# Eight conv tiles as block-product pairs in the early stage, and low parts of the scan's weights by accumulating DMA

## The chip, the cores and the metric

The kernel runs on one core of a Trainium2 chip. Its engines are TensorE (PE in the profile, with its weight loads as PEld), VectorE (DVE), ScalarE (ACT), GpSimd (POOL) and SyncE (SP); SP, ACT and POOL also issue DMAs, each from a queue of its own. Each engine works through its instructions in order. The metric is the device time of one execution in microseconds. A measurement of this kernel can tell a difference of about 0.3% from none.

## The reference

One layer of a hybrid encoder on 1024 tokens of 1024 channels. Cut to what matters here:

```
u     = rms_norm(x) * (1 + scale1) + shift1
gl, cb, cc, cx, z, xbc, dt = split(u @ w_in)
y_conv = cb * causal_conv3(cc * cx)                  # 8 tiles of 128 channels
xbc   = silu(causal_conv4(xbc) + b)                  # 32 tiles: xs, bs, cs
y     = ssd_scan(xs * dt, dt * a, bs, cs) + d_skip * xs   # 8 groups of 4 heads
y     = group_rms(y * silu(z)) * w
merged = sigmoid(gl0) * (y_conv @ w_conv_out) + sigmoid(gl1) * (y @ w_ssm_out)
x     = x + gate1 * (merged @ w_o)
x     = x + gate2 * (relu(u2 @ w_up)^2 @ w_down);  out = rms_norm(x)
```

`y_conv` needs three projections for each of its eight 128-channel tiles: `cc`, `cx` and `cb`. The scan needs four `xbc` tiles for each of its eight groups.

## The kernel before

All matrix work is done in float32 split into a high and a low part, each in the fast float32 format: a product is three matmuls (high x high, high x low, low x high). Weights come in tiles of 128 partitions x 1024 from HBM. `load_w` (L91 to L98) loads one into `wraw` (three buffers, queue of SP), casts it on ScalarE to the high part `whi`, and subtracts on VectorE for the low part `wlo` (four buffers each).

There are two ways to do a projection. `proj` (L119) takes one weight tile and all 1024 tokens: 8 row blocks x 2 halves of 512 tokens x 3 products (`mm3`, L111), which is 48 matmuls of 512 columns. `strassen_pair` (L136) takes two weight tiles and makes 2 x 2 blocks of them and of `u`; seven block products of 12 matmuls each (`prod`, L141) give the two output tiles, 84 matmuls instead of 96. It needs sums and differences of the blocks of `u`, `T1` to `T4`, made once before the early stage and held in SBUF (pools `tk0` to `tk3`); the sums of weight blocks are made on VectorE for each pair (`s12`, `s34`).

The stages, in order:

- Start: `u` from `x` and the conditioning, and the first gate tiles.
- Early stage: pairs by `strassen_pair`. Gate tiles `gl`, then the 16 `z` tiles, then conv tiles 0 to 3 (L483 to L508): for two conv tiles, one pair each gives `cx` and `cc`, whose product `v` goes through the three taps (`taps`, L477), and a third pair gives the two `cb` tiles. Results go to DRAM, the conv tiles to `yc_d`. Then the `T` blocks are released.
- Scan stage: `proj_group(g)` (L561) makes the four `xbc` tiles of a group with `xbc_tile` (L547): `proj` of one weight tile, copy to `raw` behind three zero columns that POOL sets each time, four taps, silu. `ssd_group(g)` (L573) goes through 8 chunks of 128 tokens: matmuls A (L580 to L583), B (L603, L608) and C (L625), small steps on VectorE and ScalarE between them, and a state passed from chunk to chunk. At the end of a group `zs` is multiplied by the result and POOL stores it to `y_d` (L645). `finish` sums squares.
- The loop over groups (L692 on) issues `ssd_group(g)`, then `proj_group(g + 1)`, and for g = 1 to 4 `conv_tile` (L671): conv tiles 4 to 7, each by three `proj`, with its own `ccs` and `vv` from pool `pcf` (two buffers).
- After the scan: all eight conv tiles are read back from `yc_d` through `ccs` (L710), split, and projected by `w_conv_out` beside the last scan group; then the output projections, the merge, `w_o`, and the two parts of the MLP. The down projection makes some low parts another way (L961, L962): ScalarE writes -1 times the raw tile, rounded to the fast format, which is minus the high part, and POOL issues a DMA that adds the raw weights from HBM to it; what is left is the low part.

What is issued when on each engine is fixed at build time: a planner takes the instructions in the order of the program as priorities, with its own estimate of their durations, and lays each engine's order down. Work that comes later in the program fills the gaps of work that comes earlier. Buffers are handed on with waits (`reuse_waits`).

Of the kernel before, what the change touches and what calls it, by code (L numbers as in the profile page):

```python
# [8 lines left out]
F32 = mybir.dt.float32  # L9
F32R = mybir.dt.float32r  # L10
I32 = mybir.dt.int32
AF = mybir.ActivationFunctionType
ALU = mybir.AluOpType
# [3 lines left out]
P = 128  # L17
T = 1024
H = 512
# [3 lines left out]
NC_ = 8  # L23
EPS = 1e-6
RSQRT_SEED = 0x5F3759DF
NYE = 4
PARTS = ((0, 512, (1, 4, 6)), (512, 256, (1, 3, 4, 6)), (768, 256, (2, 5)))

LN1, LN2, FNORM = 0, 8, 16
# [9 lines left out]
def hybrid_trunk(tc, xT, par, hrows, crow, wada1, wada2, win, wdt, wco, wso, wo, wup, wdt_, wdn, out):  # L39
    nc = tc.nc  # L40
    pe, act, dve, pool, sp = nc.tensor, nc.scalar, nc.vector, nc.gpsimd, nc.sync

    def tt(o, a, b, op, eng=dve):
        return eng.tensor_tensor(out=o, in0=a, in1=b, op=op)  # L44

    def stt(o, a, s, b, op0, op1):
        return dve.scalar_tensor_tensor(out=o, in0=a, scalar=s, in1=b, op0=op0, op1=op1)  # L47
# [4 lines left out]
    hs = [slice(0, H), slice(H, T)]  # L52

    cp = tc.alloc_tile_pool(name="const", bufs=1)
    wp = tc.alloc_tile_pool(name="weights", bufs=4)
# [29 lines left out]
    yc_d = dp.tile([8, P, T], F32, name="yc_d")  # L85

    def load_raw(src):
        raw = wp.tile([P, T], F32, name="wraw", bufs=3)
        sp.dma_start(raw, src)
        return raw  # L90

    def load_w(src, raw=None, eng=dve):
        if raw is None:
            raw = load_raw(src)
        hi = wp.tile([P, T], F32R, name="whi")
        act.copy(hi, raw)  # L96
        lo = wp.tile([P, T], F32R, name="wlo")
        tt(lo, raw, hi.bitcast(F32), ALU.subtract, eng=eng)  # L98
        return hi, lo

    def split(hi, lo, src):
        act.copy(hi, src)
        tt(lo, src, hi.bitcast(F32), ALU.subtract)
# [7 lines left out]
    def mm3(outs, wh, wl, xh, xl, start, stop):  # L111
        for o, h_, l_ in zip(outs, xh, xl):
            pe.matmul(o, lhsT=wh, rhs=h_, start=start, stop=False)  # L113
            pe.matmul(o, lhsT=wh, rhs=l_, start=False, stop=False)  # L114
        for o, h_ in zip(outs, xh):
            last_mm[0] = pe.matmul(o, lhsT=wl, rhs=h_, start=False, stop=stop)  # L116

    def proj(w, xh, xl, nk=KT, base=0, halves=(0, 1), width=H):
        wh, wl = w  # L119
        ps = [mm.tile([P, H], F32, name="mm")[:, :width] for _ in halves]  # L120
        for k in range(nk):
            c0 = base + k * P
            mm3(ps, wh[:, c0:c0 + P], wl[:, c0:c0 + P], [xh[k][h] for h in halves], [xl[k][h] for h in halves],
                k == 0, k == nk - 1)
        return ps
# [122 lines left out]
    uh = [[up.tile([P, H], F32R, name=f"uh{k}{h}") for h in (0, 1)] for k in range(KT)]  # L248
    ul = [[up.tile([P, H], F32R, name=f"ul{k}{h}") for h in (0, 1)] for k in range(KT)]
# [16 lines left out]
    for h in (0, 1):  # L266
        ps = mm.tile([P, H], F32, name="mm")
# [50 lines left out]
    for h in (0, 1):  # L318
# [3 lines left out]
        ps = ps0.tile([P, H], F32, name="st")  # L322
# [43 lines left out]
    p0.release()  # L366
    p0x.release()
    ws = [load_w(win[f]) for f in (4, 5)]
    tks, X = [], {n: [] for n in ("11", "21", "22", "T1", "T2", "T3", "T4")}
    dc1 = dcs[:, 8:12]  # L370
# [23 lines left out]
    for h in (0, 1):  # L394
        ps = ps0.tile([P, H], F32, name="st")
# [6 lines left out]
    ps = ps0.tile([P, H], F32, name="st")  # L402
# [74 lines left out]
    def taps(o, v, f):  # L477
        w0 = CONVW + 3 * f
        act.mul(o, v[:, 2:2 + T], prm[:, w0 + 2:w0 + 3])
        for j in (1, 0):  # L480
            stt(o, v[:, j:j + T], prm[:, w0 + j:w0 + j + 1], o, ALU.mult, ALU.add)

    for f0 in range(0, NYE, 2):  # L483
        ys_ = []
        for f in (f0, f0 + 1):
            y = glp.tile([P, T], F32, name="glt")
            v = pe1.tile([P, T + 32], F32, name="wv", bufs=1)
            pool.memset(v[:, 0:2], 0.0)
            keep = {}

            def v_ev(i, h, src):
                if (i, h) == (1, 1):
                    keep[0] = src
                elif (i, h) == (0, 0):
                    act.copy(y[:, hs[0]], src)
                else:
                    tt(v[:, 2 + H * h:2 + H * h + H], src, keep[0] if h else y[:, hs[0]], ALU.mult)

            strassen_pair(pe1, win[17 + 3 * f], win[16 + 3 * f], X, v_ev)
            taps(y, v, f)  # L500
            ys_.append(y)

        def y_ev(i, h, src):
            tt(ys_[i][:, hs[h]], src, ys_[i][:, hs[h]], ALU.mult)

        strassen_pair(pe1, win[18 + 3 * f0], win[21 + 3 * f0], X, y_ev)
        for i in (0, 1):
            act.dma_start(yc_d[f0 + i], ys_[i])  # L508
# [5 lines left out]
    with tc.issue_after(last_mm[0].ins):  # L514
        strict = p0e.tile([P, P], F32, name="strict")
        tsc(strict, tri, -1.0, 1.0, ALU.mult, ALU.add)
        ps = ps1.tile([P, H], F32, name="st")
        pe.matmul(ps[:, :C2], lhsT=tri, rhs=z2, start=True, stop=True)
        act.copy(acum.rearrange("p c h -> p (c h)"), ps[:, :C2])
        ps = ps1.tile([P, H], F32, name="st")  # L520
        pe.matmul(ps[:, :C2], lhsT=strict, rhs=z2, start=True, stop=True)
        pe.matmul(ps[:, C2:2 * C2], lhsT=ones, rhs=z2, start=True, stop=True)
        v = p0e.tile([P, C2], F32, name="v")
# [4 lines left out]
        for h in (0, 1):  # L528
            ps = ps1.tile([P, H], F32, name="st")
# [11 lines left out]
    p2t = tc.alloc_tile_pool(name="p2t", bufs=2, reuse_waits="tile")  # L541
    pcf = tc.alloc_tile_pool(name="pcf", bufs=2, reuse_waits="tile")
    psA = tc.alloc_tile_pool(name="psA", bufs=2, space=PSUM)
    psB = tc.alloc_tile_pool(name="psB", bufs=1, space=PSUM)
    psC = tc.alloc_tile_pool(name="psC", bufs=1, space=PSUM)

    def xbc_tile(win_i, ci, dst):  # L547
        ps = proj(load_w(win[win_i]), uh, ul)
        raw = p2t.tile([P, T + 3], F32, name="raw")
        pool.memset(raw[:, 0:3], 0.0)  # L550
        for h in (0, 1):
            act.copy(raw[:, 3 + H * h:3 + H * h + H], ps[h])
        a = p2t.tile([P, T], F32, name="cacc")
        for h in (0, 1):
            act.activation(a[:, hs[h]], ps[h], AF.Identity, bias=hb[:, ci:ci + 1], scale=hw[:, 4 * ci + 3:4 * ci + 4])  # L555
        for j in (2, 1, 0):
            stt(a, raw[:, j:j + T], hw[:, 4 * ci + j:4 * ci + j + 1], a, ALU.mult, ALU.add)
        act.activation(dst, a, AF.Tanh)
        stt(dst, dst, 1.0, a, ALU.add, ALU.mult)

    def proj_group(g):  # L561
        pg = p2g[g % 2]
        xs = pg.tile([P, 2, T], F32, name="xs")
        bf = pg.tile([P, T], F32, name="bf")
        cf = pg.tile([P, T], F32, name="cf")
        b = gtile(g)
        xbc_tile(b + 0, 2 * g, xs[:, 0, :])
        xbc_tile(b + 1, 2 * g + 1, xs[:, 1, :])
        xbc_tile(b + 2, 16 + g, bf)
        xbc_tile(b + 3, 24 + g, cf)  # L570
        return xs, bf, cf
# [96 lines left out]
        tsc(r, r, 0.5, None, ALU.mult, ALU.bypass)  # L668
        act.dma_start(rst_d[4 * i:4 * i + 4].rearrange("g (c t) -> (g c) t", t=P), r)

    def conv_tile(f):  # L671
        ccs = pcf.tile([P, T], F32, name="ccs")
        v = pcf.tile([P, T + 2], F32, name="vv")
        pool.memset(v[:, 0:2], 0.0)
        cps = proj(load_w(win[16 + 3 * f]), uh, ul)
        for h in (0, 1):
            act.copy(ccs[:, hs[h]], cps[h])
        xps = proj(load_w(win[17 + 3 * f]), uh, ul)
        for h in (0, 1):
            tt(v[:, 2 + H * h:2 + H * h + H], xps[h], ccs[:, hs[h]], ALU.mult)  # L680
        taps(ccs, v, f)
        bps = proj(load_w(win[18 + 3 * f]), uh, ul)
        for h in (0, 1):
            tt(ccs[:, hs[h]], bps[h], ccs[:, hs[h]], ALU.mult)
        act.dma_start(yc_d[f], ccs)

    def drive(gen):
        try:
            next(gen)
            return None  # L690
        except StopIteration as e:
            return e.value  # L692
# [3 lines left out]
    for g in range(NG - 1):  # L696
        gen = ssd_group(g, *cur, prev)
        prev = None
        while prev is None:
            prev = drive(gen)  # L700
        cur = proj_group(g + 1)
        if g in (1, 2, 3, 4):
            conv_tile(NYE + g - 1)
    up.release()

    yy = tc.alloc_tile_pool(name="yy", bufs=8, side="right", reuse_waits="tile")
    yc = []
    for f in range(8):
        ccs = pcf.tile([P, T], F32, name="ccs")
        sp.dma_start(ccs, yc_d[f])  # L710
        y = yy.tile([P, 2, T], F32R, name="ys")
        split(y[:, 0, :], y[:, 1, :], ccs)
        yc.append(y)
# [6 lines left out]
    for f in range(8):  # L720
# [3 lines left out]
        ps = proj(load_w(wco[f]), ych, ycl)  # L724
# [9 lines left out]
    for b in range(4):  # L734
# [18 lines left out]
        for f in range(8):  # L753
            if f % 2 == 0:
                w = load_w(wso[b, f // 2])
            if b == 0:
# [5 lines left out]
                ps = proj(w, yh, yl, nk=4, base=(f % 2) * 512)  # L762
# [10 lines left out]
            ps = proj(w, yh, yl, nk=4, base=(f % 2) * 512)  # L773
# [30 lines left out]
    for h in (0, 1):  # L804
        st = Stats(p6, pst, pool, 7)
        for f in range(8):
            x_ = xp.tile([P, H], F32, name=f"x{f}{h}")
            sp.dma_start(x_, xT[f, :, hs[h]])
            ps, = proj(load_w(wo[f]), mh, ml, halves=(h,))
# [12 lines left out]
    for h in (0, 1):  # L822
        for i in range(4):
            ps, = proj(ws[i], u2h, u2l, halves=(h,))
# [82 lines left out]
    for f in range(8):  # L907
# [4 lines left out]
        ps = proj(w, hh, hl, nk=4, base=(f % 2) * 512)  # L912
# [9 lines left out]
    for s in range(3):  # L922
# [26 lines left out]
        for n, blk in enumerate((0, 2, 5, 4, 3, 1, 6)):  # L949
            t = operand([lambda q=q: stage(op_d[s, 2 * q:2 * q + 2, :, blk, :].rearrange("k p t -> p k t")) for q in (0, 1)])  # L950
            first = n in (0, 2, 3, 5)
            for q in (0, 1):
                wh = wp.tile([P, T], F32R, name="whi")
                wl = wp.tile([P, T], F32R, name="wlo")
                for i in (0, 1):
                    val, src = piece(n, 2 * q + i)
# [29 lines left out]
    for t0, tw, onpool in PARTS:  # L986
        h, o = t0 // H, t0 % H
# [3 lines left out]
        for f in range(8):  # L991
            ps, = proj(ws[f // 2], [[v[h][:, win_]] for v in hh], [[v[h][:, win_]] for v in hl],
                       nk=4, base=(f % 2) * 512, halves=(0,), width=tw)
# [83 lines left out]
```

## Time and profile before

| what | value |
|---|---|
| median of 3 runs | 2125.92 us (2124.54 to 2130.34) |
| the profiled execution | 2126.34 us |
| its span, first to last instruction | 2124.3 us |
| mean granted TensorE clock | 0.989 |
| last block products of the early stage | 482.75 us |
| first scan matmul (A of group 0) | 543.06 us |
| end of the store of group 6's `zs`, issue | 1119.02 us |

A row of a group reads: line, engine, operation, output <- inputs, shape, count | busy time, mean ns of one | idle time of its engine before it and what ended it. Line 44, 47 and 50 are helpers (`tt`, `stt`, `tsc`), so groups are told apart by the names of their tiles. In the timeline a row is start, duration, engine, line and operation, with the idle time before it in brackets. A PE row's duration is longer than the interval to the next, since matmuls are pipelined.

### The profile page before, as it was taken

Reading aid. Unit: us, or ns where it says so; the run is one execution under the profiler, and the core shown is the slowest. Engines: PE = TensorE matmul, PEld = TensorE weight load, DVE = VectorE, ACT = ScalarE, POOL = GpSimd, SP = SyncE. Lnnn points to the kernel's source line nnn. Section 1 sums busy time; section 2 is a strip of 40 time slices with the busy share of each in tenths; the row PEclk is TensorE's granted clock in tenths of the full one; section 3 lists DMA queues with packets and bytes.
Section 4 is the critical chain, followed back from the end, with each engine's and each line's share of the span. In section 5 each row is a group of like instructions: output and inputs, shape, how many; then the busy total and the mean of one; then the engine's idle time right before and its main releaser. Section 6 shows DMA issues by size and latency. Waiting matters only on the chain.

```text
span 2124.3 us, 26250 instructions
## 1 busy us (share of the span) xinstructions
PE 2089.6 (98%) x9776; PEld 1705.5 (80%) x9776; DVE 1474.3 (69%) x2278; ACT 927.4 (44%) x1554; POOL 152.3 (7%) x242
## 2 busy tenths in 40 slices
PE   7999999999999999999999999999999999999998
PEld 4778888888888887888877888888888888888887
DVE  7866888665786757576786558845866665668674
ACT  4433333224565636364664231233544454544432
POOL 0000000000000000000000000011000001232213
PEclk8999999999999999999999999999999999999998
DMA  8226554223133223232337586453144347988932
GB/s 302 80 100 200 189 189 165 71 80 122 60 100 110 85 90 85 95 115 80 104 121 262 189 299 201 159 203 124 65 164 159 145 162 261 304 241 254 275 77 80
DMA packets 133617, 327.32 MB, mean 154 GB/s; under 512 B 12481, under 2 KB 47681, under 8 KB 131954
## 3 DMA queue, kind: packets, MB, share of 16 engines
q1 hardware_dynamic: 98978, 202.76, 29.4%
q0 software_dynamic: 22240, 87.04, 12.9%
q10 hardware_dynamic: 12272, 35.85, 4.3%
q8 instruction: 77, 1.26, 0.2%
q14 instruction: 50, 0.41, 0.1%
HBM read 253.05 MB, written 72.55 MB: 153 GB/s over the span
## 4 chain that ended last, share of the span: by engine, by line
PE 82%; issue 10%; DVE 4%; DMA 2%; POOL 1%; ACT 1%; SPq 0%; DVEq 0%; POOLq 0%; ACTq 0%
PE mm L147 21%; PE mm L116 15%; PE mm L113 15%; PE mm L114 15%; PE mm L971 9%; PE B L603 2%; PE B L608 1%; PE C L625 1%; DMA wv<-in_wada 1%; DVE wada L294 1%; PE A L580 1%; DMA x<-in_xT 1%; POOL wv L418 1%; DVE ul L47 1%; DVE x L47 0%
## 5 line engine op out<-in xcount | busy, mean ns | idle before, releaser
L113 PE MATMUL mm<-uh,whi 128*128 128x512 f32 x768 | 303.0, 398 | 3.7 <-ACT uh L106 3.2
L114 PE MATMUL mm<-ul,whi 128*128 128x512 f32 x768 | 304.8, 397 | 0.0
L147 PE MATMUL mm<-t,whi 128*128 128x512 f32 x944 | 290.5, 390 | 0.9 <-DVE cq L44 0.9
L116 PE MATMUL mm<-uh,wlo 128*128 128x512 f32 x768 | 246.4, 396 | 1.9 <-DVE wlo L44 1.9
L96 ACT CAST whi<-wraw 128x1024 fp32r<-128x1024 f32 x101 | 106.1, 1050 | 261.9 <-PE mm L114 219.9
L44 DVE TENSOR_TENSOR wlo<-wraw,whi 128x1024 fp32r<-128x1024 f32 (+1 forms) x167 | 186.6, 1118 | 37.4 <-ACT whi L96 31.3
L147 PEld LDWEIGHTS mm<-t,whi 128*128 128x128 f32 x944 | 176.9, 188 | 39.1 <-DVE cq L44 2.4
L971 PE MATMUL mm<-op,whi 128*128 128x512 f32 x672 | 207.2, 389 | 1.0 <-DVE y L47 0.9
L147 PE MATMUL mm<-t,wlo 128*128 128x512 f32 x472 | 183.0, 389 | 0.0
L113 PEld LDWEIGHTS mm<-uh,whi 128*128 128x128 f32 x768 | 144.5, 189 | 35.6 <-ACT uh L106 4.9
L116 PEld LDWEIGHTS mm<-uh,wlo 128*128 128x128 f32 x768 | 144.9, 189 | 32.2 <-DVE wlo L44 2.3
L114 PEld LDWEIGHTS mm<-ul,whi 128*128 128x128 f32 x768 | 145.0, 189 | 29.4 <-issue 0.9
L113 PE MATMUL mm<-ys,whi 128*128 128x512 f32 x384 | 148.9, 397 | 2.3 <-DVE gt L47 1.8
L44 DVE TENSOR_TENSOR wlo<-s,whi 128x1024 fp32r<-128x1024 f32 (+1 forms) x114 | 112.0, 995 | 54.4 <-ACT whi L152 53.6
L114 PE MATMUL mm<-ys,whi 128*128 128x512 f32 x384 | 149.1, 396 | 0.0
L971 PEld LDWEIGHTS mm<-op,whi 128*128 128x128 f32 x672 | 126.0, 188 | 28.1 <-ACT whi L957 1.3
L47 DVE SCALAR_TENSOR_TENSOR cacc<-raw,hw,cacc 128x1024 f32<-128x1024 f32 x96 | 122.9, 1280 | 27.6 <-ACT cacc L555 27.2
L147 PE MATMUL mm<-s,whi 128*128 128x512 f32 x448 | 138.3, 389 | 0.7 <-ACT cu L170 0.7
L971 PE MATMUL mm<-op,wlo 128*128 128x512 f32 x336 | 130.7, 389 | 0.0
L597 ACT ACTIVATE seg<-acb,acum 128x128 f32<-128x128 f32 x256 | 81.9, 392 | 98.7 <-PE B L603 88.6
L47 DVE SCALAR_TENSOR_TENSOR y<-mm,mcol,y 128x512 f32<-128x512 f32 (+1 forms) x100 | 69.4, 706 | 77.6 <-PE mm L971 39.4
L116 PE MATMUL mm<-ys,wlo 128*128 128x512 f32 x384 | 122.5, 394 | 0.0
(280 smaller groups left out, 4080.9 us busy)
## 6 DMA issues: line engine op xcount, KB each, us to landing
wraw<-in_win SPq DMA_DIRECT2D x87, 512.0 KB, 3.5
dr<-in_wdt_ SPq DMA_DIRECT2D x108, 256.0 KB, 5.8
op_d<-hp POOLq DMA_DIRECT2D x12, 1792.0 KB, 6.0
hr<-op_d POOLq DMA_DIRECT2D x42, 512.0 KB, 6.3
wv<-in_wada POOLq DMA_DIRECT2D x32, 512.0 KB, 3.8
acb<-ac_d SPq DMA_DIRECT2D x64, 256.0 KB, 4.5
wraw<-in_wup SPq DMA_DIRECT2D x32, 512.0 KB, 3.5
gt<-gl_d SPq DMA_DIRECT2D x24, 512.0 KB, 4.4
```

The costliest lines, as they stand in the source:

```text
L44: return eng.tensor_tensor(out=o, in0=a, in1=b, op=op)
L47: return dve.scalar_tensor_tensor(out=o, in0=a, scalar=s, in1=b, op0=op0, op1=op1)
L96: act.copy(hi, raw)
L113: pe.matmul(o, lhsT=wh, rhs=h_, start=start, stop=False)
L114: pe.matmul(o, lhsT=wh, rhs=l_, start=False, stop=False)
L116: last_mm[0] = pe.matmul(o, lhsT=wl, rhs=h_, start=False, stop=stop)
L147: last_mm[0] = pe.matmul(o, lhsT=l_[:, s_], rhs=r_, start=first and k == j == 0, stop=k == 3 and j == 2, skip_group_check=True)
L294: return dve.tensor_tensor_reduce(out=w_, in0=w_, in1=cb, scale=0.5, scalar=prm[:, BADA + o:BADA + o + 1], op0=ALU.mult, op1=ALU.add, accu ...
L418: pool.dma_start(w_, wada2[i])
L597: act.activation(seg[:, r, :], acb[:, r, :], AF.Relu, bias=acum[:, c, hd:hd + 1], scale=-1.0)
L603: pe.matmul(Bk[o:o + 64, P * (r // 2):P * (r // 2) + P], lhsT=xd[:, r, :], rhs=seg[:, r, :], start=True, stop=True, skip_group_check=True)
L971: pe.matmul(o, lhsT=l_[:, c_], rhs=t[:, r_, k, :], start=first and k == j == 0, stop=k == 3 and j == 2, skip_group_check=True)
```

## The change

- The early loop over conv tiles runs over all eight (12 pairs instead of 6); `conv_tile` and its four calls between the scan groups go.
- `xbc_tile` takes its weights by a new `load_w_acc`: the low part is written by ScalarE as -1 times the raw tile in the fast format, and a DMA from POOL's queue adds the raw tile from HBM to it. The subtraction on VectorE goes, for 32 weight tiles.
- The raw tiles of `xbc_tile` are two fixed ones, used in turn, whose three zero columns are set once.
- `ccs` has three buffers for the read-back of the conv tiles, and `vv` goes.

```
+    def load_w_acc(src):
+        raw = load_raw(src)
+        hi = wp.tile([P, T], F32R, name="whi")
+        act.copy(hi, raw)
+        lo = wp.tile([P, T], F32R, name="wlo")
+        act.mul(lo, raw, -1.0)
+        pool.dma_start(lo, src, accum_op=ALU.add)
+        return hi, lo
...
-    for f0 in range(0, NYE, 2):
+    for f0 in range(0, 8, 2):
...
+    padded = [p2t.tile([P, T + 3], F32, name=f"raw{i}", bufs=1) for i in (0, 1)]
+    for raw in padded:
+        pool.memset(raw[:, 0:3], 0.0)
+    padded = itertools.cycle(padded)
+
     def xbc_tile(win_i, ci, dst):
-        ps = proj(load_w(win[win_i]), uh, ul)
-        raw = p2t.tile([P, T + 3], F32, name="raw")
-        pool.memset(raw[:, 0:3], 0.0)
+        ps = proj(load_w_acc(win[win_i]), uh, ul)
+        raw = next(padded)
...
-    def conv_tile(f):
-        ccs = pcf.tile([P, T], F32, name="ccs")
-        v = pcf.tile([P, T + 2], F32, name="vv")
-        pool.memset(v[:, 0:2], 0.0)
-        cps = proj(load_w(win[16 + 3 * f]), uh, ul)
...
-        xps = proj(load_w(win[17 + 3 * f]), uh, ul)
...
-        taps(ccs, v, f)
-        bps = proj(load_w(win[18 + 3 * f]), uh, ul)
...
-        act.dma_start(yc_d[f], ccs)
...
         cur = proj_group(g + 1)
-        if g in (1, 2, 3, 4):
-            conv_tile(NYE + g - 1)
...
     for f in range(8):
-        ccs = pcf.tile([P, T], F32, name="ccs")
+        ccs = pcf.tile([P, T], F32, name="ccs", bufs=3)
         sp.dma_start(ccs, yc_d[f])
```

More of the change, by code (lines that the diff above doesn't have):

```diff
@@ L25 @@
 RSQRT_SEED = 0x5F3759DF
-NYE = 4
 PARTS = ((0, 512, (1, 4, 6)), (512, 256, (1, 3, 4, 6)), (768, 256, (2, 5)))
@@ L669, in rstd @@
         act.dma_start(rst_d[4 * i:4 * i + 4].rearrange("g (c t) -> (g c) t", t=P), r)
-    def conv_tile(f):
-        ccs = pcf.tile([P, T], F32, name="ccs")
-        v = pcf.tile([P, T + 2], F32, name="vv")
-        pool.memset(v[:, 0:2], 0.0)
-        cps = proj(load_w(win[16 + 3 * f]), uh, ul)
-        for h in (0, 1):
-            act.copy(ccs[:, hs[h]], cps[h])
-        xps = proj(load_w(win[17 + 3 * f]), uh, ul)
-        for h in (0, 1):
-            tt(v[:, 2 + H * h:2 + H * h + H], xps[h], ccs[:, hs[h]], ALU.mult)
-        taps(ccs, v, f)
-        bps = proj(load_w(win[18 + 3 * f]), uh, ul)
-        for h in (0, 1):
-            tt(ccs[:, hs[h]], bps[h], ccs[:, hs[h]], ALU.mult)
-        act.dma_start(yc_d[f], ccs)
     def drive(gen):
```

## The prediction

> **What bounds the kernel now.** I read the page first: the span, the busy shares, the slices and the chain.
>
> ```profile
> span 2124.3 us, 26250 instructions
> PE 2089.6 (98%) x9776; PEld 1705.5 (80%) x9776; DVE 1474.3 (69%) x2278; ACT 927.4 (44%) x1554; POOL 152.3 (7%) x242
> ...
> PEclk8999999999999999999999999999999999999998
> ...
> PE 82%; issue 10%; DVE 4%; DMA 2%; POOL 1%; ACT 1%; SPq 0%; DVEq 0%; POOLq 0%; ACTq 0%
> ```
>
> TensorE is busy 98% of the span at full granted clock, and carries 82% of the chain that ended last. The mean could hide a stage with another limit, and the change moves work between two stages, so the second view is the table by stretches of time. Its columns are: stretch, length, then the busy time of PE, PEld, DVE, ACT and POOL with their counts, granted clock, DMA share and GB/s. The first row holds nearly six of today's conv pairs in the early stage, the next two the first two scan groups, then a dense part of group 3, the conv tile after it, and two short stretches at the end of the scan stage, where `yc` is taken over.
>
> ```profile
> 377.00:490.00 113.00, 113.00 (x500) 93.59 (x499) 75.02 (x94) 32.68 (x38) 0.63 (x7) 1.00 0.26 85
> 543.00:612.00 69.00, 69.00 (x383) 56.23 (x383) 58.18 (x110) 39.36 (x87) 0.50 (x5) 1.00 0.24 69
> 612.00:680.00 68.00, 68.00 (x362) 54.35 (x361) 51.85 (x91) 42.59 (x89) 1.47 (x6) 1.00 0.32 99
> 787.00:850.00 63.00, 63.00 (x343) 50.42 (x342) 48.59 (x88) 40.09 (x86) 0.94 (x5) 1.00 0.27 76
> 850.00:882.00 32.00, 32.00 (x147) 26.65 (x147) 14.92 (x21) 8.33 (x11) 0.53 (x1) 1.00 0.33 115
> 1085.00:1090.00 5.00, 3.75 (x30) 2.72 (x26) 4.58 (x12) 4.95 (x12) 0.00 (x0) 1.00 0.07 19
> 1090.00:1095.00 5.00, 3.38 (x15) 2.13 (x16) 4.97 (x9) 5.00 (x11) 0.00 (x0) 0.80 0.54 162
> ```
>
> PE has no gap in the early pairs, in the scan groups or in the conv tile between them: in each of those rows its busy time is the length of the stretch. Only the last two rows have idle time (1.25 and 1.62 us). The waits of PE over the scan stage and the handover, 470 to 1200 us, say the same; the columns are total, times, longest.
>
> ```profile
> PE mm L113 <- DVE gt L47: 1.8, 1, 1.8
> PE C L660 <- DVE sql L44: 1.4, 1, 1.4
> PE B L603 <- DVE seg L44: 1.0, 1, 1.0
> PE mm L113 <- ACT ys L102: 0.5, 1, 0.5
> ```
>
> That is 4.7 us in 730. So a matmul removed is worth its issue interval, and time taken off VectorE is worth nothing by itself. "Busy" is modelled, so I check the interval in the timeline of PE (start, duration):
>
> ```profile
> 577.16 0.62 PE L116 MATMUL mm<-uh,wlo 128*128 128x512 f32 x2
> 577.61 0.39 PE L113 MATMUL mm<-uh,whi 128*128 128x512 f32 x1
> 577.84 0.39 PE L114 MATMUL mm<-ul,whi 128*128 128x512 f32 x1
> 578.07 0.39 PE L113 MATMUL mm<-uh,whi 128*128 128x512 f32 x1
> 578.29 0.39 PE L114 MATMUL mm<-ul,whi 128*128 128x512 f32 x1
> 578.52 0.62 PE L116 MATMUL mm<-uh,wlo 128*128 128x512 f32 x2
> ```
>
> Six 512-column matmuls start between 577.16 and 578.52 us, one every 0.227 us, though each is listed at 0.39. The early pairs keep the same pace: 113.00 us for 500 is 0.226. I use 0.227 for both.
>
> **The change: conv tiles.** A conv tile of the scan stage is three projections, each 8 row blocks x 2 halves x 3 products: 144 matmuls, 32.7 us. The row 850 to 882 is such a tile, 32 us with little beside it. Four go: 576 x 0.227 = 130.8 us. Two more passes of the early loop come: six pairs of 7 products x 12 matmuls, 504 x 0.227 = 114.4 us. Net: 72 matmuls, **-16.3 us**. The loads of the 12 weight tiles and the four stores of `yc` move with them, on the same SP and ACT queues; POOL's four short memsets of `v` move too. The early rows have DMA share 0.26, VectorE at 75.0 of 113 and ScalarE at 32.7 of 113, and the added pairs repeat the pattern that is there, with PE gapless. So I add nothing there.
>
> **The change: low parts.** The groups of instructions (count, busy in all, mean ns of one, idle before) give the trade for one weight tile:
>
> ```profile
> L44 DVE TENSOR_TENSOR wlo<-wraw,whi 128x1024 fp32r<-128x1024 f32 x134 | 164.0, 1224 | 37.4 <-ACT whi L96 31.3 <-ACT whi L152 4.1
> L96 ACT CAST whi<-wraw 128x1024 fp32r<-128x1024 f32 x101 | 106.1, 1050 | 261.9 <-PE mm L114 219.9 <-PE mm L147 17.9 <-PE mm L971 16.4
> L962 POOL DMA_DIRECT2D wlo<-in_wdt_ x36 | 32.5, 1025 | 47.4 <-ACT wlo L961 47.4
> ...
> wlo<-in_wdt_ POOLq DMA_DIRECT2D x36, 256.0 KB, 7.3
> ...
> DMA to landing us min/median/max: 4.1/7.3/11.7
> ```
>
> One 1.22 us subtraction leaves VectorE, 32 times (39 us). For each, ScalarE gets a multiplication by -1, for which I take the 1.05 us of its cast of the same tile, and POOL issues an accumulating DMA. The nearest rows are those of the down projection: 1.03 us on POOL on the mean and 7.3 us to landing, for half the bytes. In the dense stretch 787 to 850, about four weight tiles pass: VectorE would fall from 48.6 to 43.7 of 63 us, ScalarE rise from 40.1 to 44.3. Both stay below PE's 63.0. The value on the path is 0, both ways, as long as the low parts come in time.
>
> In time means this. Four weight buffers let the cast run up to three projections ahead of use, at least 3 x 48 x 0.227 = 32.7 us. Multiplication, issue and the longest landing above take 1.05 + 1.03 + 11.7 = 13.8 us after the cast; 18.9 us of cover remain. The cover is missing in one place, the first tile after the pairs:
>
> ```profile
> 472.07 1.05 ACT L96 CAST whi<-wraw 128x1024 fp32r<-128x1024 f32 x1 [4.32 <-PE mm L147]
> ...
> 484.35 0.40 PE L116 MATMUL mm<-uh,wlo 128*128 128x512 f32 x1
> ...
> 483.00:490.00 7.00, 7.00 (x32) 5.81 (x31) 2.67 (x5) 1.32 (x2) 0.00 (x0) 1.00 0.94 313
> ```
>
> The cast ends at 473.1, the multiplication at 474.2, POOL at 475.2. With 4.1 us the low part lands at 479.3, with 7.3 at 482.5, with 11.7 at 486.9, and PE needs it at 484.35: between 0 and 2.6 us lost. The tile here is twice the size and the DMA share from 483 on is 0.94, so I take a value near the upper end, **+2 us**; behind this tile the others have 10.9 us more each. The Trainium skill, DMA: Bandwidth & Descriptors, section "Anatomy of one DMA — SWDGE (gpsimd) path", has a POOL-issued DMA take about 2.0 us plus the bytes at 436 KB per us, an estimate of 3.2 us for this 512 KB tile. By it the tile lands at 478.4, this term is 0 and the sum is 2 us lower. The trace's accumulating DMAs took more than twice that for half the bytes, and none landed under 4.1, so the measured rows decide.
>
> **The change: padded tiles.** 32 memsets of three columns become two. Their need is order, not time: POOL is in order, and each memset waited for a tap on VectorE.
>
> ```profile
> POOL raw L550 <- DVE cacc L47: 482.3, 28, 49.8
> POOL y_d L645 <- DVE zs L44: 72.7, 14, 54.3
> ```
>
> An accumulating DMA behind such a memset would have waited up to 49.8 us. With the memsets gone, only the stores of `y` stand in that queue and wait, for the end of a group. Value 0; the second row is kept for a rival.
>
> **The change: `yc` loads.** Three buffers instead of two. At the handover ScalarE waited for these loads:
>
> ```profile
> ACT ys L102 <- DMA ccs<-yc_d: 5.5, 5, 1.9
> ```
>
> PE idles 2.9 us from 1085 to 1095, and the clock of 0.80 in the second half costs another 1.0. Mostly VectorE's order (`sql`, `seg` above) did that, so I take 0, with bounds of -3.9 (all of it goes) and +3.9 (it comes twice).
>
> **Sum.** The profiled execution took 2126.34 us, 2.0 more than its span and 0.4 above the median 2125.92. 2126.3 - 16.3 + 2 = **2112.0**. Against the median it would be 2111.6; I keep 2112.
>
> **Rivals.** The conv tiles also were cover for PE at the turn from one group to the next. The end of a group and the start of the next, from the timelines of PE and VectorE:
>
> ```profile
> 595.57 1.22 DVE L47 SCALAR_TENSOR_TENSOR cf<-cf,cacc 128x1024 f32<-128x1024 f32 x1
> ...
> 600.51 0.38 PE L580 MATMUL A<-cf,bf 128*128 128x128 f32 x2
> ...
> 610.53 2.35 DVE L44 TENSOR_TENSOR zs<-xs,zs 128x1024 f32<-128x1024 f32 x2
> ...
> 779.17 0.38 PE L580 MATMUL A<-cf,bf 128*128 128x128 f32 x2
> ...
> 847.94 2.36 DVE L44 TENSOR_TENSOR zs<-xs,zs 128x1024 f32<-128x1024 f32 x2
> ```
>
> *Groups in series (slower).* Group 3 runs from 779.17 to 850.3, 71.1 us, while PE's work in its dense part is 63.0. If without conv tiles the groups follow one another end to start, PE loses 8.1 us at each of the six turns between groups 0 and 6: 48.6, so 2126.3 - 14.3 + 48.6 = 2161. It decides against the change from 14.3 / 6 = 2.4 us a turn. Against it: between groups 0 and 1, where no conv tile stands today, group 1's first matmul (600.51) starts 10 us before group 0's last multiplication (610.53), 4.9 us after the last step of its own `cf` began (595.57), and PE is full through the whole stretch 543 to 680. For it: only that turn shows it, and the two `xs` buffers allow no more than one group ahead. Chance 0.10.
>
> *Low parts late (no change).* An accumulating DMA queued behind a `y` store waits for `zs`. If the store is placed 21 us too early, the cover of 18.9 is used up and PE loses some 2 us in each of seven groups: 2112 + 14 = 2126; from 1 to 3 us a group, 2119 to 2133. For it: POOL stood up to 54.3 us before a store. Against: in the down projection 36 such DMAs share POOL's queue with other waiting DMAs, and the order of the queue follows a planner's time, in which a store is issued when its data are due. Chance 0.15.
>
> **How the numbers follow.** Forecast 0.75, its own range 2126.3 - 16.3 - 3.9 = 2106 to 2112 + 3.9 = 2116. The low-parts case reaches from there over 2126; half of it, to 2123, is taken in with a third of a loss at the turns. Range 2106 to 2123. A measurement of this kernel tells about 0.3%, 6.4 us, from no change. Faster: 0.75, plus 0.04 for low parts barely late: 0.79. Same: 0.11 of the low-parts case and 0.01 of the turns: 0.12. Slower: 0.09.
>
> **What would show it.** Right: 72 fewer matmuls on PE; the early stage 114 us longer, the stage from 483 us on some 131 us shorter; groups about 62 to 63 us apart, PE's busy time equal to the length of each stretch; VectorE's share of the scan groups near 70%. A first wait of PE on `wlo` of a few us near 600 us would confirm the +2. Wrong: waits of PE on `wlo` in every group (low parts late), or PE idle with lowered clock around each `zs` (series); or gaps in the six added pairs, where I allowed none.

## The result and the profile after

The changed kernel takes 2108.76 us (median of 6 runs, 2107.74 to 2115.09), the kernel before 2125.38 in the same comparison. The ratio is 0.993, 95% interval 0.9919 to 0.9942: 12 to 17 us less. The profiled execution took 2108.83 us. All ratios here are of fast executions alone; one execution of the last experiment, of 8.9 ms, is left out. The same lines of the changed kernel's page:

```profile
span 2107.1 us, 26132 instructions
PE 2070.9 (98%) x9704; PEld 1689.8 (80%) x9704; DVE 1482.6 (70%) x2312; ACT 962.8 (46%) x1600; POOL 177.4 (8%) x244
...
PE 86%; issue 7%; DVE 4%; DMA 2%; POOL 1%; ACT 1%; SPq 0%; DVEq 0%; POOLq 0%; ACTq 0%
```

TensorE has 72 matmuls less (9704 against 9776) and 18.7 us less busy time, and carries the chain as before. Where the 17.2 us of span went is read between three marks that both traces have: the last matmul of a pair, the last matmul on conv or scan outputs (`ys`), and the end. The last pair matmul, from the timeline of PE after the change (482.75 before), and the rows of `ys` before and then after; the time behind "to" is the last start.

```profile
598.20 0.40 PE L155 MATMUL mm<-t,wlo 128*128 128x512 f32 x1
```

```profile
L116 PE MATMUL mm<-ys,wlo x384: 387/389/632, 1095.4 to 1382.1; 128*128 128x512 f32 x192
```

```profile
L124 PE MATMUL mm<-ys,wlo x384: 387/389/628, 1070.4 to 1367.2; 128*128 128x512 f32 x192
```

To the last pair it takes 598.20 - 482.75 = 115.4 us more. From there to the last `ys` matmul it was 1382.1 - 482.75 = 899.4 and is 1367.2 - 598.20 = 769.0: 130.4 less. The rest, which nothing in the change touches, is 742.2 and 739.9. The sum is -17.2, which is the whole difference of the spans.

The table by stretches of the kernel after, with the early pairs, three stretches of scan groups, and the handover to the conv projections:

```profile
368.80:598.40 229.60, 229.60 (x1014) 190.13 (x1013) 153.85 (x198) 69.40 (x81) 2.84 (x10) 1.00 0.24 78
660.00:720.00 60.00, 60.00 (x336) 48.54 (x336) 44.52 (x88) 39.71 (x82) 2.90 (x4) 1.00 0.46 101
900.00:960.00 60.00, 60.00 (x330) 48.36 (x331) 48.49 (x90) 43.04 (x89) 4.60 (x6) 1.00 0.54 137
960.00:1020.00 60.00, 60.00 (x322) 48.08 (x321) 49.20 (x95) 42.62 (x88) 4.59 (x6) 1.00 0.57 141
1060.00:1065.00 5.00, 3.83 (x31) 2.65 (x29) 4.73 (x8) 5.00 (x10) 0.00 (x1) 1.00 0.44 175
1065.00:1070.00 5.00, 1.35 (x4) 0.82 (x5) 5.00 (x10) 5.00 (x8) 0.00 (x0) 0.84 0.49 154
1070.00:1075.00 5.00, 5.00 (x13) 3.91 (x12) 5.00 (x6) 4.96 (x13) 0.00 (x0) 0.50 0.74 231
```

The twelve pairs and the scan groups are still gapless on TensorE. VectorE is at 74 to 82% in the groups, more than the 70% that was foretold. All idle time from 600 to 1250 us is at the handover to the conv projections: 1.17 and 3.65 us, and then 5 us at half clock. The waits of PE over scan stage and handover name it:

```profile
PE mm L121 <- ACT ys L110: 3.7, 1, 3.7
PE mm L122 <- DVE ys L43: 1.1, 1, 1.1
```

No wait on a low part stands there.

So the sum came out by the matmul count. Whether the other part of the change, the low parts, is worth nothing, as the sum had it, the traces can't say: it must be taken away.

### The profile page after: what moved, and what is told of

Its sections match the earlier page's. It is cut to its first block, busy times and chain, and to the rows that moved or that the text cites. A ratio compares the mean times of both kernels' runs of the same rounds, so it can differ in the third digit from the quotient of the medians.

```text
span 2107.1 us, 26132 instructions
## 1 busy us (share of the span) xinstructions
PE 2070.9 (98%) x9704; PEld 1689.8 (80%) x9704; DVE 1482.6 (70%) x2312; ACT 962.8 (46%) x1600; POOL 177.4 (8%) x244
## 4 chain that ended last, share of the span: by engine, by line
PE 86%; issue 7%; DVE 4%; DMA 2%; POOL 1%; ACT 1%; SPq 0%; DVEq 0%; POOLq 0%; ACTq 0%
PE mm L155 26%; PE mm L124 14%; PE mm L122 14%; PE mm L121 14%; PE mm L965 11%; PE B L615 2%; PE B L620 2%; PE C L637 1%; DMA wv<-in_wada 1%; DVE wada L302 1%; PE A L592 1%; POOL wv L426 1%; DMA x<-in_xT 1%; DVE ul L46 1%; DVE x L46 0%
## 5 line engine op out<-in xcount | busy, mean ns | idle before, releaser
L155 PE MATMUL mm<-t,whi 128*128 128x512 f32 x1136 | 349.8, 390 | 1.6 <-DVE cq L43 1.6
L121 PE MATMUL mm<-uh,whi 128*128 128x512 f32 x576 | 228.0, 400 | 3.7 <-ACT uh L114 3.2
L122 PE MATMUL mm<-ul,whi 128*128 128x512 f32 x576 | 229.7, 399 | 0.0
L155 PE MATMUL mm<-t,wlo 128*128 128x512 f32 x568 | 220.4, 389 | 0.0
L124 PE MATMUL mm<-uh,wlo 128*128 128x512 f32 x576 | 185.3, 396 | 1.9 <-DVE wlo L43 1.9
L43 DVE TENSOR_TENSOR wlo<-wraw,whi 128x1024 fp32r<-128x1024 f32 (+1 forms) x135 | 144.1, 1068 | 15.3 <-ACT whi L95 8.9
L46 DVE SCALAR_TENSOR_TENSOR cacc<-raw,hw,cacc 128x1024 f32<-128x1024 f32 x96 | 122.7, 1278 | 38.5 <-ACT cacc L567 37.9
L121 PEld LDWEIGHTS mm<-uh,whi 128*128 128x128 f32 x576 | 108.4, 189 | 28.3 <-ACT uh L114 5.3
L124 PEld LDWEIGHTS mm<-uh,wlo 128*128 128x128 f32 x576 | 108.0, 189 | 24.2 <-DVE wlo L43 2.3
L122 PEld LDWEIGHTS mm<-ul,whi 128*128 128x128 f32 x576 | 109.0, 189 | 21.6 <-issue 0.5
L160 ACT CAST whi<-s 128x1024 fp32r<-128x1024 f32 x78 | 81.8, 1050 | 96.2 <-PE mm L155 95.2
```

The lines of the kernel that those rows point to most:

```text
L155: last_mm[0] = pe.matmul(o, lhsT=l_[:, s_], rhs=r_, start=first and k == j == 0, stop=k == 3 and j == 2, skip_group_check=True)
```

## The experiments

Two theories. *Matmul count*: TensorE is the bound before and after, the pairs give the gain, the low parts nothing. *VectorE needs the relief*: without conv tiles between the groups, the scan can't keep up unless VectorE is relieved. A third, that the accumulating DMAs cost something, stands beside them. Ratios are against the kernel before, measured beside each group of runs, with 95% intervals; 0.001 is 2.1 us.

| run | ratio | interval |
|---|---|---|
| the change | 0.9930 | 0.9919 to 0.9942 |
| pairs only | 1.0040 | 1.0024 to 1.0056 |
| low parts only | 1.0002 | 0.9991 to 1.0014 |
| half of the conv tiles | 0.9946 | 0.9926 to 0.9965 |
| raw tile cleared each time | 0.9924 | 0.9907 to 0.9941 |
| extra subtraction | 1.0007 | 0.9994 to 1.0020 |
| low parts on GpSimd | 0.9963 | 0.9949 to 0.9977 |
| half of the low parts | 0.9988 | 0.9975 to 1.0000 |
| pairs only, third `xs` | 0.9963 | 0.9952 to 0.9974 |
| the change, third `xs` | 0.9952 | 0.9938 to 0.9965 |
| the change, two `ccs` | 0.9953 | 0.9938 to 0.9968 |
| first casts on GpSimd | 0.9934 | 0.9917 to 0.9950 |
| four tiles split early | 0.9933 | 0.9913 to 0.9953 |

**Pairs only**

```
 def xbc_tile(win_i, ci, dst):
-    ps = proj(load_w_acc(win[win_i]), uh, ul)
-    raw = next(padded)
+    ps = proj(load_w(win[win_i]), uh, ul)
+    raw = p2t.tile([P, T + 3], F32, name="raw")
+    pool.memset(raw[:, 0:3], 0.0)
```

> The changed kernel, but the scan's low parts by the subtraction on VectorE and the raw tile cleared for each use, as before: only the conv tiles move (and the third ccs buffer). Theory 'matmul count' (TensorE is the bound before and after, the low parts are worth nothing by themselves): 72 matmuls at 0.227 us less than the kernel before, -16 us, about 2109, the same as the changed kernel within 2 us; no wait of TensorE on the scan's low parts or on VectorE in the scan groups. Rival 'VectorE needs the relief': without conv tiles the scan groups come every 61 us with VectorE at about 48 of 60 us; four subtractions more make 53, and TensorE begins to wait for VectorE in the groups: at least 5 us slower than the changed kernel, 2114 or more. Rival 'the accumulating DMAs cost something': faster than the changed kernel, 2105 or less, most of it at the handover to the conv projections.

2135.8 us, 1.0040 of the kernel before: slower. The pairs without the low parts lose 8 us where the count gives 16. The matmul count as a full account falls with this run. Stretches of its table by time:

```profile
840.00:900.00 60.00, 60.00 (x318) 48.38 (x317) 47.87 (x82) 35.85 (x74) 1.46 (x6) 1.00 0.33 100
900.00:960.00 60.00, 53.49 (x295) 42.71 (x294) 47.62 (x92) 38.62 (x86) 1.46 (x6) 0.94 0.31 94
960.00:1020.00 60.00, 60.00 (x322) 47.77 (x321) 49.03 (x97) 37.31 (x81) 1.27 (x4) 1.00 0.32 93
1020.00:1080.00 60.00, 54.13 (x297) 43.41 (x295) 47.23 (x89) 36.28 (x78) 0.40 (x4) 0.96 0.33 93
1080.00:1090.00 10.00, 3.54 (x20) 2.61 (x19) 7.60 (x11) 4.59 (x7) 1.07 (x2) 0.67 0.95 333
1090.00:1100.00 10.00, 3.38 (x8) 2.70 (x9) 9.82 (x15) 9.04 (x15) 0.00 (x0) 0.50 0.19 58
```

TensorE now stops for 6.5 us inside the groups (939 to 947 us), for 5.9 us from 1071 us on, and for 13.1 us more at the handover, and the clock falls with it. The second stop already lies behind the last projection matmul, which starts at 1069.2 us: by then no projection is left beside the scan. The two largest of TensorE's waits over the scan stage and the handover:

```profile
PE mm L121 <- ACT cacc L563: 16.7, 2, 11.9
PE C L633 <- DVE xe L43: 4.1, 2, 2.9
```

VectorE isn't full in any stretch of 60 us. So what is short? The timelines give it. Of VectorE, in the run with pairs only: the last step of a group's projections (`cf`) and the end of its scan (`zs`), for groups 0 and 3:

```profile
653.04 1.23 DVE L46 SCALAR_TENSOR_TENSOR cf<-cf,cacc 128x1024 f32<-128x1024 f32 x1 [1.18 <-ACT cf L566]
726.35 2.36 DVE L43 TENSOR_TENSOR zs<-xs,zs 128x1024 f32<-128x1024 f32 x2
...
832.30 1.21 DVE L46 SCALAR_TENSOR_TENSOR cf<-cf,cacc 128x1024 f32<-128x1024 f32 x1
937.42 2.35 DVE L43 TENSOR_TENSOR zs<-xs,zs 128x1024 f32<-128x1024 f32 x2
```

From start to start, group 0's `zs` comes 73.3 us after its `cf`, group 3's 105.1 us after: the scan falls behind the projections by 10.6 us a group. This distance is called the lag below. There are two sets of `xs` buffers. When the scan is about 105 us behind, the projections of the group after next (here group 5) have nowhere to go. Right behind that `zs`, in the timelines of ACT and PE:

```profile
940.73 1.99 ACT L566 ACTIVATE xs<-cacc 128x1024 f32<-128x1024 f32 x2
...
946.36 1.44 ACT L563 ACTIVATE cacc<-mm,hb,hw 128x512 f32<-128x512 f32 x2
...
947.19 0.79 PE L121 MATMUL mm<-uh,whi 128*128 128x512 f32 x1 [4.85 <-ACT cacc L563]
```

By the program `xs` of group 5 can be written only once `zs` of group 3 has read the old one. ScalarE writes it 1.0 us after that `zs` ends; the PSUM banks (TensorE's output buffers) are emptied after that (`cacc`); TensorE waited 4.85 us for them. The 11.9 us wait at the handover ends with a `cacc` too, behind group 7's `xs`; ScalarE also waited 4.6 and 1.3 us for loads of `yc` just before, so the buffers need not be its only cause. The `cf` and `zs` rows in the kernel after, groups 0 and 5:

```profile
654.57 1.23 DVE L46 SCALAR_TENSOR_TENSOR cf<-cf,cacc 128x1024 f32<-128x1024 f32 x1 [1.18 <-ACT cf L570]
725.84 2.35 DVE L43 TENSOR_TENSOR zs<-xs,zs 128x1024 f32<-128x1024 f32 x2
...
953.16 1.22 DVE L46 SCALAR_TENSOR_TENSOR cf<-cf,cacc 128x1024 f32<-128x1024 f32 x1
1056.79 2.35 DVE L43 TENSOR_TENSOR zs<-xs,zs 128x1024 f32<-128x1024 f32 x2
```

71.3 us behind at group 0, 103.6 at group 5: 6.5 a group, and the limit is met only when the projections are at their end. In the kernel before, the lag began at the same 73.3 us, but a conv tile after the projections of each of groups 2 to 5 gave the scan some 32 us to catch up. Its rows for groups 2 and 5:

```profile
653.48 1.22 DVE L47 SCALAR_TENSOR_TENSOR cf<-cf,cacc 128x1024 f32<-128x1024 f32 x1
753.25 2.35 DVE L44 TENSOR_TENSOR zs<-xs,zs 128x1024 f32<-128x1024 f32 x2
...
945.33 1.22 DVE L47 SCALAR_TENSOR_TENSOR cf<-cf,cacc 128x1024 f32<-128x1024 f32 x1
1037.33 2.35 DVE L44 TENSOR_TENSOR zs<-xs,zs 128x1024 f32<-128x1024 f32 x2
```

The lag is 99.8 us at group 2 and 92.0 at group 5: with a conv tile for each group it no longer grows. This became the theory *lag*: the scan's chain is longer than TensorE's work for a group, VectorE's load sets by how much, and the buffers set when TensorE feels it. One thing the runs leave open: the order on each engine is fixed at build time and planned anew for every run, so they show that the lag grows with VectorE's load under this planner, not that no other order of the same work would keep it smaller.

**Low parts only**

```
-    ps = proj(load_w(win[win_i]), uh, ul)
-    raw = p2t.tile([P, T + 3], F32, name="raw")
-    pool.memset(raw[:, 0:3], 0.0)
+    ps = proj(load_w_acc(win[win_i]), uh, ul)
+    raw = next(padded)
```

(in the kernel before, with `load_w_acc` and the two fixed raw tiles, and its conv tiles where they were)

> The kernel before, with the scan's low parts by accumulating DMA and the two fixed raw tiles, and the conv tiles left between the scan groups. Theory 'matmul count': no change, 2125 within 2 us, VectorE's busy time 39 us lower, ScalarE's 34 higher. Rival 'VectorE needs the relief': a gain of more than 3 us already here. Rival 'the accumulating DMAs cost something': 3 us or more slower, with waits of TensorE on a low part.

1.0002: no change, within 3 us. With conv tiles between the groups the relief buys nothing. Its worth depends on the other half of the change.

**Half of the conv tiles**

```
-NYE = 4
+NYE = 6
...
-        if g in (1, 2, 3, 4):
+        if g in (1, 2):
```

> The kernel before with conv tiles 4 and 5 moved into the early loop and 6 and 7 left between the scan groups; low parts on VectorE. Theory 'matmul count': 36 matmuls at 0.227 us less, -8.2 us, about 2117. Rival 'cover': the conv tiles also fill TensorE at the turns of the groups, and the second half of the dose, which takes the last cover away, gives less than the first; then this run gains as much as the one with all conv tiles moved, or more.

2115.65 us, 0.9946: -11.5 us, interval -7 to -16, which holds the -8.2 of the count. Without the low parts, half of the added pairs gain and all of them lose: the second half costs some 20 us, as *cover* said. By the rows of pairs only it does so through the lag and not at the turns.

**Raw tile cleared each time**

```
-        raw = next(padded)
+        raw = p2t.tile([P, T + 3], F32, name="raw")
+        pool.memset(raw[:, 0:3], 0.0)
```

> The changed kernel, but POOL clears the three columns of a new raw tile for each of the 32 scan tiles, in the same queue as the accumulating DMAs. Theory of the prediction: weights are cast up to three projections ahead, 32.7 us, and 18.9 us of it are left after the low part's own path; a clearing that waits for taps on VectorE (up to 49.8 us before the change) ahead of an accumulating DMA uses that up in some groups: TensorE waits on low parts, 3 to 15 us slower than the changed kernel, 2112 to 2124. Rival 'order by planned time': the queue's order puts each DMA where its data are due, and the two fixed tiles change nothing: 2109 within 2 us.

0.9924, the same as the change within the intervals, and no wait of TensorE on a low part. The fixed raw tiles are worth nothing that this run can tell. The prediction's reason for them, that a clearing would hold up the DMAs behind it by up to 49.8 us, is not borne out.

**An extra subtraction**

```
         pool.dma_start(lo, src, accum_op=ALU.add)
+        junk = pcf.tile([P, T], F32R, name="wjunk", bufs=1)
+        tt(junk, raw, hi.bitcast(F32), ALU.subtract)
```

> The changed kernel with its low parts by DMA, and beside them the old subtraction on VectorE once more for each of the 32 scan tiles, into a tile that nothing reads. It gives VectorE its old load back and nothing else. Theory 'lag' (the scan's chain of a group takes longer than TensorE needs for a group's matmuls, so it falls behind the projections a few us per group, and the two buffer sets stop the projections when it is two groups behind; VectorE's time sets the chain's pace): like the run with pairs only, about 2135, at least 2125, with zs about 70 us apart and TensorE idle near 920 to 1100 us. Rival 'weight path' (the subtraction hurts because weights wait in VectorE's queue, not by its time): the weights come by DMA here, so 2109 within 4 us.

2126.6 us, 1.0007: above the 2125 that *lag* asked for, though short of its 2135. 32 steps of 1.22 us that nobody reads take 0.0077 (16 us) away, all of the change's gain. The longest of TensorE's waits after 590 us:

```profile
PE C L639 <- DVE xe L43: 7.4, 2, 4.6
PE mm L123 <- ACT cacc L569: 3.4, 1, 3.4
```

They are on scan steps and on the full buffers, and none in that list is on weights. Pairs only lose 7 us more (1.0040), with intervals that don't touch; there the subtraction also stands in the way of the weights. That this is what the 7 us are was not tested alone.

**Low parts on GpSimd**

```
-    ps = proj(load_w(win[win_i]), uh, ul)
+    ps = proj(load_w(win[win_i], eng=pool), uh, ul)
```

(in pairs only)

> Pairs only, with the scan's 32 subtractions on GpSimd in place of VectorE; no accumulating DMA. A 512 column addition takes 1.54 us there, so about 3 us for one of 1024, 98 us in all on an engine that is idle. Theory 'lag': VectorE is relieved as in the changed kernel, and the time is the same, 2109 within 4 us. Rival 'shared reads': VectorE's own two-input steps of the scan get longer beside GpSimd's (their mean durations rise), and most of the gain is lost: 2118 or more. Rival 'it is the DMA': as with pairs only, about 2135.

2116.8 us, 0.9963, between *lag* (2113 at most) and *shared reads* (2118 or more). Without any accumulating DMA some 16 of the 23 us that part pairs only from the change are back, so it isn't the DMA as such. But 7 us are missing. TensorE has no stop of a microsecond inside the groups in this run, and 10.3 us at the handover against 4.8 in the kernel after. What *shared reads* said of VectorE's steps is in the groups of instructions, of the kernel after:

```profile
L43 DVE TENSOR_TENSOR seg<-seg,smk 128x512 f32<-128x512 f32 x64 | 43.6, 683 | 3.5 <-ACT seg L610 2.9
L46 DVE SCALAR_TENSOR_TENSOR xs<-xs,prm,t 128x128 f32<-128x128 f32 x112 | 34.0, 344 | 0.5
L43 DVE TENSOR_TENSOR t<-B,ebc 128x256 f32<-128x256 f32 x56 | 23.5, 420 | 8.3 <-PE B L620 8.2
```

and of this run:

```profile
L43 POOL TENSOR_TENSOR wlo<-wraw,whi 128x1024 fp32r<-128x1024 f32 x32 | 82.3, 2573 | 167.9 <-ACT whi L95 152.1 <-PE mm L124 11.8 <-ACT cacc L563 2.3
L43 DVE TENSOR_TENSOR seg<-seg,smk 128x512 f32<-128x512 f32 x64 | 47.6, 745 | 3.1 <-ACT seg L606 2.8
L46 DVE SCALAR_TENSOR_TENSOR xs<-xs,prm,t 128x128 f32<-128x128 f32 x112 | 40.9, 405 | 0.4
L43 DVE TENSOR_TENSOR t<-B,ebc 128x256 f32<-128x256 f32 x56 | 23.4, 418 | 17.3 <-PE B L616 17.2
```

VectorE's steps with two inputs in SBUF are 9% and 18% longer on the mean (in pairs only they are 684 and 345 ns, as in the kernel after), the one with an input in PSUM is not. The Trainium skill, SBUF — State Buffer, section "Who interferes with whom", says that a VectorE instruction with two SBUF inputs contends with a GpSimd instruction that reads SBUF; these rows agree. That the longer steps are the whole of the 7 us was not tested: GpSimd's subtraction is also twice as long as VectorE's.

**Half of the low parts**

```
-        ps = proj(load_w_acc(win[win_i]), uh, ul)
+        ps = proj((load_w if ci < 16 else load_w_acc)(win[win_i]), uh, ul)
```

> The changed kernel with accumulating DMAs for the B and C tiles of each group only; the two xs tiles of a group are subtracted on VectorE again. Theory 'lag': VectorE gets 2.4 us per group back, the lag grows by some 2 us per group more than in the changed kernel and reaches the limit of the buffers near the last groups only: between, 2112 to 2124, nearer to the changed kernel than to pairs only, since the loss starts only where the buffers end. A loss in proportion (13 of 27 us, 2122) would speak for a steady loss per tile instead.

2121.96 us, 0.9988: 12 us of the gain gone, half of what all 32 cost, at the upper end of *lag* and just what a loss in proportion gives. It did not lie nearer to the changed kernel, which *lag* expected, so by time alone this run does not tell the two apart. By place it does: TensorE has no steady loss but stops where it does in pairs only, 5.4 us at 942 to 949 us, where the lag has reached 107 us at group 3, and 9.5 us from 1074 us on.

**Pairs only with a third `xs`**

```
+    p2x = tc.alloc_tile_pool(name="p2x", bufs=3, reuse_waits="tile")
...
-        xs = pg.tile([P, 2, T], F32, name="xs")
+        xs = p2x.tile([P, 2, T], F32, name="xs")
...
-        ccs = pcf.tile([P, T], F32, name="ccs", bufs=3)
+        ccs = pcf.tile([P, T], F32, name="ccs")
```

> Pairs only, with a third buffer for the two xs tiles of a group (and ccs with two, to make room). VectorE has its full load. Theory 'lag' with the buffers as the limit: the projections may run one group further ahead, the stops of TensorE inside the scan stage (6.5 us near 930, 5.9 us after 1020) go, and part of the loss: 2115 to 2130. Rival 'VectorE is simply too slow': the buffers change when it stops and not how much, 2135 within 3 us.

2118.1 us, 0.9963: 16 us come back with VectorE's work untouched. The stretch in which pairs only had stopped, and `cf` and `zs` of group 5, from the table by stretches and the timeline of VectorE:

```profile
900.00:960.00 60.00, 60.00 (x328) 48.66 (x327) 51.20 (x89) 39.14 (x84) 1.47 (x6) 1.00 0.33 101
...
951.87 1.22 DVE L46 SCALAR_TENSOR_TENSOR cf<-cf,cacc 128x1024 f32<-128x1024 f32 x1
...
1073.87 2.35 DVE L43 TENSOR_TENSOR zs<-xs,zs 128x1024 f32<-128x1024 f32 x2
```

No stop, and the scan is 122.0 us behind, past the 105 at which TensorE stopped before. The lag is there; the buffers let it grow. With this the buffer limit is shown as the place where the lag becomes time. The idle time that is left lies at the handover, behind the last projection matmul (1056.3 us), 8.4 us of it in waits for ScalarE's casts of `yc`.

**The change with a third `xs`**: the same edit in the changed kernel.

> The changed kernel with a third buffer for the two xs tiles of a group, and ccs with two. Theory 'lag': in the changed kernel zs trails its group's cf by 71 us at group 0 and 104 at group 5, just under the two groups at which the projections stop, so TensorE has no stop in the scan groups that a third buffer could remove: no change against the changed kernel, 2109 within 3 us, and a lag at group 6 no smaller than its 126 us. Rival 'buffers bind there too': 2105 or less.

0.9952, no faster: no stop in the groups was left to remove, as *lag* said. At 2115.9 us it is outside the expected 2109 within 3, and its lag at group 6 is 122.7 us, a little under the expected 126. It also has two `ccs` buffers, and the next run, with that alone, has the same ratio. Beside pairs only with a third `xs` (0.9963) it says more: with three `xs` buffers the low parts by DMA are worth about 2 us, within the intervals, where with two sets they are worth 23.

**The change with two `ccs`**

```
-        ccs = pcf.tile([P, T], F32, name="ccs", bufs=3)
+        ccs = pcf.tile([P, T], F32, name="ccs", bufs=2)
```

> The changed kernel with two buffers for the read-back of the conv tiles, as before. The prediction took the third buffer at 0, between -3.9 and +3.9 us. Theory: the handover's 3.7 us wait of TensorE is for ScalarE's cast of the first tile, whose data have long landed, so one buffer less changes nothing there: 2109 within 2 us. Rival: the loads pace the first conv projections, 3 us or more slower.

0.9953 against 0.9930, with intervals that just overlap: 0 to some 9 us, and outside the expected 2109 within 2. But the read-back is not where the profiled execution loses them. The wait for ScalarE's first cast is the same 3.7 us with two. The run's first scan matmul starts at 662.37 us against 658.51 in the kernel after, 3.9 us late and long before any `yc` is read back, and at the first `ys` matmul it is still 3.9 us late (1071.4 against 1067.5). Why a buffer count of the handover moves the start of the scan stage stays open.

**First casts on GpSimd**, and **four tiles split early**: two tries at the handover.

```
-        split(y[:, 0, :], y[:, 1, :], ccs)
+        if f < 3:
+            pool.tensor_copy(y[:, 0, :], ccs)
+            tt(y[:, 1, :], ccs, y[:, 0, :].bitcast(F32), ALU.subtract)
+        else:
+            split(y[:, 0, :], y[:, 1, :], ccs)
```

> The changed kernel with the high parts of the first three conv tiles cast on GpSimd at the handover in place of ScalarE. There TensorE waits 3.7 us for ScalarE's first cast, 1.1 for VectorE's subtraction, and the clock falls to 0.84 and 0.50 for 5 us each: 4.8 idle and 3.3 of clock, 8.1 us in all. Theory 'ScalarE's backlog': TensorE starts on the conv tiles earlier, 3 to 8 us faster than the changed kernel, 2101 to 2106. Rival 'VectorE's backlog': VectorE is busy for all of 1065 to 1090 us, the low part of the first tile comes no sooner, and GpSimd's reads lengthen VectorE's steps: 2109 within 2 us, or slower.

0.9934, no change within the interval. The wait moved from ScalarE's cast to VectorE's low part:

```profile
PE mm L122 <- DVE ys L43: 4.6, 3, 3.3
```

```
+            yhi = pe1.tile([P, T + 32], F32R, name="wv", bufs=1)[:, 0:T]
+            split(yhi, ys_[i], ys_[i])
+            act.dma_start(ysp_d[f0 - 2 + i, :, 0], yhi.bitcast(F32))
+            act.dma_start(ysp_d[f0 - 2 + i, :, 1], ys_[i])
...
+        if 2 <= f < 6:
+            pool.dma_start(y, ysp_d[f - 2])
```

> The changed kernel, with conv tiles 2 to 5 split into high and low part in the early stage (where ScalarE is busy 30% and VectorE 67%), stored split, and read back at the handover straight into their operand tiles by four DMAs of 1 MB from GpSimd's queue; tiles 0, 1, 6 and 7 as in the changed kernel. It takes four of the eight casts and subtractions, 9.1 us of work, out of the handover. Theory 'the handover's backlog on ScalarE and VectorE': TensorE there lost 4.8 us idle and 3.3 us of clock in the changed kernel; with less queued, 2 to 6 us faster than the changed kernel, 2103 to 2107, and VectorE no longer busy for all of 1065 to 1090. Rival 'the space': the operand tiles lie where u lay, so nothing can start before the last projection is through, and 4 MB of DMA then take 13 us beside other loads: TensorE waits for a DMA in place of ScalarE, 2109 or slower. Rival 'early cover': the split beside the pairs stops TensorE there: the early stage longer than 114 us by some us.

0.9933, no change either, with an interval too wide to see 4 us. TensorE still waited 3.7 us for the first cast, which is tile 0's, and that tile was not among the four. No version here is measurably faster than the change.

## Why the prediction was right, and the step that was not

- **Conv tiles, -16.3 us.** Right, in both halves: 115.4 us added where 114.4 was forecast, 130.4 removed where 130.8 was.
- **Low parts, "the value on the path is 0, both ways".** This step failed, although the sum held. Alone they are worth 0 (1.0002). With the pairs they are worth 0.0110, 23 us: without them the change is slower than the kernel before. I compared VectorE's busy time with TensorE's in one dense stretch of the kernel before. But that stretch was followed by 32 us of conv tile in which the scan caught up. Busy shares below 100% did not show that the chain through VectorE ran longer than TensorE's work for a group. The sum held since the lag of the changed kernel reaches 103.6 us at group 5, just short of the 105 at which pairs only stopped. I had worked out no such margin: that part is luck.
- **First low part, +2 us.** It was 0: the DMA was issued at 589.84 us, needed at 599.80, and there is no wait. The forecast of 2112.0 is 3.2 us above the profiled execution: 2.0 are this term, 2.3 lie behind the last `ys` matmul, which the change doesn't touch, and the pairs give 1.0 back.
- **Padded tiles, 0.** Right, but the two tiles weren't needed for it: clearing each tile costs nothing that the run can tell.
- **Third `ccs` buffer, 0 with bounds of 3.9.** As a price of the handover 0 was right: TensorE lost as much there as before, 4.8 us idle plus 3.4 of clock against 4.7 plus 3.4. But the prediction's 3.9 us for the kernel before was too small, and so were its bounds. It left out the lower clock behind 1095 us, and the later stop with its clock, the 1.8 us wait for `gt` that it lists. In the table of the kernel before:

```profile
1095.00:1100.00 5.00, 5.00 (x20) 4.08 (x19) 3.54 (x4) 4.50 (x11) 0.00 (x0) 0.86 0.83 275
1125.00:1130.00 5.00, 3.74 (x11) 2.93 (x12) 5.00 (x9) 4.37 (x11) 0.00 (x0) 0.72 0.76 251
```

- **Rival in series.** The groups did not go in series: in the kernel after the spacing of `zs` is 64 to 69 us up to group 5, above the 62 to 63 that was foretold. But the danger it named was real, and its evidence against, a full TensorE from 543 to 680 us, held only for the first two groups. A lag that grows by 6 to 11 us a group shows at the fourth. My chance of 0.10 was fair for the change as made, and would have been far too low for the pairs alone.
- **Rival low parts late.** No: 32 accumulating DMAs, no wait of TensorE on one.

## What to carry to other kernels

A gapless engine shows that the filler is used, not that the chain beside it would keep up without it: before taking filler out, read how far one stage trails the other from group to group, and against how many buffers. Of two edits made together, one can be worth nothing alone and be what makes the other pay, so a term of zero has to be asked for in the company of the other edits.

## What the runs showed of the hardware

The accumulating DMAs of 512 KB from GpSimd's queue took longer to land than the plain ones of that size in the same queue, which took 3.8 us on the median for `wv` and 5.7 for `hr`:

```profile
L106 POOL DMA_DIRECT2D wlo<-in_win x32: 850/859/892, 589.8 to 1005.9; - x32
...
DMA to landing us min/median/max: 6.5/7.7/13.8
```

The estimate of 3.2 us that the prediction worked out from the Trainium skill (DMA: Bandwidth & Descriptors, section "Anatomy of one DMA — SWDGE (gpsimd) path") is less than half of this median; the measurement decides. And with 32 subtractions on GpSimd beside them, VectorE's steps with two inputs in SBUF were 9 to 18% longer on the mean of the run, as shown above.
